# Front of a hybrid attention / SSD block: rotary tables in a pool of their own, a quarter of the first FOX weights in a lasting pool, transposes tied one tile late

## The chip, the cores and the metric

The kernel runs on one core of a Trainium2 chip. The metric is the device time of one execution in microseconds (us); the kernel before takes 2170.09 us (median of 3 runs, 2169.45 to 2170.87). Engines are named as the profile names them: PE is TensorE, DVE is VectorE, ACT is ScalarE, POOL is GpSimd, SPq is the queue on which every DMA of this kernel is issued. Each engine works through its own instruction list in order and waits where an operand or a buffer is not ready.

## The reference

One layer, 1024 tokens of width 1024, float32. The change lies in the front: the norm, the low-rank projections of the latent attention (MLA), its per-head q, k and v, and the projections of the forgetting attention (FOX) and of z.

```python
hn = rms_norm(x, norm_mix_g[l])
u = hn @ w_in[l]                       # split into u_mla (672), u_fox (1544), u_ssm, u_gate
# latent attention, before its softmax
c_q, c_kv, k_rope = jnp.split(u, [384, 640], axis=-1)
q  = (rms_norm(c_q, q_norm_g) @ w_uq).reshape(B, S, 8, 96)
kv = (rms_norm(c_kv, kv_norm_g) @ w_ukv).reshape(B, S, 8, 128)
k_nope, v = jnp.split(kv, [64], axis=-1)
k = jnp.concatenate([k_nope, broadcast(k_rope)], axis=-1)
q = rope_tail(rms_norm(q, q_gain), cos, sin)
k = rope_tail(rms_norm(k, k_gain), cos, sin)
# forgetting attention, before its softmax
q, k, v, f_raw = jnp.split(u, [512, 1024, 1536], axis=-1)
q = rms_norm(q.reshape(B, S, 8, 64), q_gain)
k = rms_norm(k.reshape(B, S, 8, 64), k_gain)
# SSD branch: z, xBC, dt_raw = split(u_ssm); its output is multiplied by silu(z)
...
```

The three branches are then attended or scanned, gated, merged and projected, and a gated MLP with a depthwise convolution follows. None of that is touched.

## The kernel before

Every fp32 product is made of three fp32r matmuls: each operand is split into a high part (ACT copies it, rounding to fp32r) and a low part (DVE subtracts the high part from the source), and `mm3` (L156) issues high x high, high x low, low x high for each of the 128-row slices k of the contraction. A weight is therefore loaded (`raw`), split by ACT and DVE, and only then used.

Tokens are handled in NT = 8 tiles of 128. The front has these stages.

Stage 1, loop at L366, over tiles t. `norm_tile` (L171) normalizes tile t+2, transposes it on PE (`pt`, 8 transposes) and splits it into `hnh`, `hnl`. Then 24 matmuls make `cq` (384 columns) and 24 make `ckv` (312 columns). ACT squares them, DVE makes the two reciprocal roots and writes the normalized row `cn` (L391, L393; one buffer). Five PE transposes of `cn` (L398, in groups of 3 and 2) go to `ch[t]`, `cl[t]`. In the iteration t = 5, `rope_and_columns` (L218) computes the rotary tables on POOL from `rt` tiles and loads and transposes four parameter blocks through one `pr` buffer (`pcp`, `pcn`). Its tiles come from the pool `ap`, which also holds `xt`, `xn`, `xg` and the gain.

PSUM has 8 banks here: 4 with the tag `mm`, 2 with `mv`, 2 with `tp`. `cq`, `ckv`, `q`, `kv` take `mm`; all the transposes take `tp`; the two `tp` buffers go round in the order of the program text.

Between the stages the pool `ap` closes and `upp`, the pool of the MLA up-projection weights (`uqh`, `uql`, `ukh`, `ukl`), takes its place on the right side of SBUF. Its raw pieces pass through five `raw` buffers of stage 1 (L341).

Stage 2, loop at L446: for each tile 18 matmuls give `q`, 12 give `kv`. ACT evacuates and squares them (`sq`, `sqk`), DVE reduces and makes the roots, POOL applies the rotation, and 16 PE transposes (L495) yield the rows that are stored to DRAM (`q_h`, `q_l`, `k_h`, `k_l`).

Stage 3, loop at L505: the FOX v columns in two halves of 256. Each half loads its weights (`load_cols`, one buffer set) and does 24 matmuls for each tile into an `mv` bank. ACT and DVE split the result into `fv` (one buffer), which is stored (`fv_d`, L514). The scheduler interleaves the first half's matmuls with stage 2.

Stage 4, loop at L636: 32 units of 24 matmuls of 512 columns, in the order z first half, FOX q, FOX k, z second half, 8 tiles each. `load512` (L613) fills `w5h`, `w5l` in four pieces of two k slices each through two `wr` buffers of the pool `fill`, which opens at L517 on the right side where `upp` was. A z unit ends in a tanh and a store; a q or k unit in a square, a reduction, the reciprocal root (`fv8`, `fr8`), the product `fqn` and four PE transposes (L668).

After that come the two attentions with their fill work (lines 683 to 1240), the merge and output projection, and the MLP.

The order on each engine up to the end of the merge is not written out: a list scheduler with a timeline simulation decides at compile time which ready instruction an engine takes next, and that order is then fixed. Pools opened with `reuse_waits="tile"` make a tile wait only for the earlier tiles whose bytes it takes over. In the allocation of the kernel before, `ukl` lies on bytes of `xg` and of the rotary tables, and the first `wr` buffer lies on bytes of the two `sl` tiles of stage 2.

Of the kernel before, what the change touches and what calls it, by code (L numbers as in the profile page):

```python
# [21 lines left out]
P = 128  # L22
# [15 lines left out]
def f32(ap):  # L38
    return ap.bitcast(F32)
# [3 lines left out]
def block_kernel(ctx: ExitStack, tc: tile.TileContext, x, positions, norm_mix_g, w_in, b_gate,  # L43
# [83 lines left out]
    def uid(s):  # L127
        cnt[0] += 1
        return f"{s}_{cnt[0]}"

    def split(h, l, src, he=None, le=None):
# [5 lines left out]
            he.tensor_copy(h, src)  # L137
        le.tensor_sub(l, src, f32(h))  # L138

    def rsqrt(pool, y, v, n):  # L140

        yi = pool.tile([P, n], I32, name=uid("rs_i"), tag="rs_i")
        V.tensor_single_scalar(yi, v.bitcast(I32), 1, op=ALU.logical_shift_right)
        V.tensor_scalar(y.bitcast(I32), yi, -1, RSQRT_MAGIC, op0=ALU.mult, op1=ALU.add)
        vh = pool.tile([P, n], F32, name=uid("rs_v"), tag="rs_v")
        V.tensor_scalar_mul(vh, v, -0.5)
        for _ in range(3):
            t = pool.tile([P, n], F32, name=uid("rs_t"), tag="rs_t")
            if n == 1:
                V.scalar_tensor_tensor(out=t, in0=y, scalar=y, in1=vh, op0=ALU.mult, op1=ALU.mult)  # L150
            else:
                V.tensor_mul(t, y, y)
                V.tensor_mul(t, t, vh)
            V.scalar_tensor_tensor(out=y, in0=t, scalar=1.5, in1=y, op0=ALU.add, op1=ALU.mult)

    def mm3(ps, lh, ll, rh, rl, nk):  # L156

        n = 3 * nk
        i = 0
        for k in range(nk):  # L160
            for a, b in ((lh, rh), (lh, rl), (ll, rh)):
                T.matmul(ps, a(k), b(k), start=(i == 0), stop=(i == n - 1))  # L162
                i += 1


    def alloc_hn():
# [163 lines left out]
    with ExitStack() as p0:  # L330
        mp = p0.enter_context(TP("mp0", 2))
        pa = ExitStack()
        ap_ = pa.enter_context(TP("ap", 2, side="right"))
        xts = []
        gmix = None

        def wsplit(pool, tag, shape, pieces):
            h = pool.tile(shape, F32R, name=tag + "h", tag=tag + "h", bufs=1)
# [27 lines left out]
        for t in range(NT):  # L366
            if t + 3 < NT:
                load_x(t + 3)
            if t + 2 < NT:
                norm_tile(ap_, "xn", mp, psp, xts[t + 2], gmix, hnh, hnl, t + 2, "tp")  # L370
            if t == NT - 3:
                rope_and_columns(ap_)
            th, tl = tok(hnh, t), tok(hnl, t)
            p1 = acc("cq")
            mm3(p1[:, :384], th, tl, lambda k: w1h[:, k, :], lambda k: w1l[:, k, :], NK)
            p2 = acc("ckv")
            mm3(p2[:, :312], th, tl, lambda k: w2h[:, k, :], lambda k: w2l[:, k, :], NK)
# [12 lines left out]
            cn = mp.tile([P, 640], F32, name=uid("cn"), tag="cn", bufs=1)  # L390
            V.scalar_tensor_tensor(out=cn[:, 0:384], in0=p1[:, :384], scalar=r[:, 0:1], in1=gcq,  # L391
                                   op0=ALU.mult, op1=ALU.mult)
            V.scalar_tensor_tensor(out=cn[:, 384:640], in0=p2[:, :256], scalar=r[:, 1:2], in1=gckv,  # L393
                                   op0=ALU.mult, op1=ALU.mult)
            for k0, k1 in ((0, 3), (3, 5)):
                pt = tps()
                for k in range(k0, k1):
                    T.transpose(pt[:, k - k0, :], cn[:, k * P:(k + 1) * P], ident)  # L398
# [22 lines left out]
    with ExitStack() as pm:  # L421
# [21 lines left out]
            eng.tensor_add(dst[:, :, 16:32], t3, t4)  # L443

        vcols = [load_cols(fvp, "v", C_FQ + 1024, 256, 1)]
        for t in range(NT):  # L446

            qn = mp.tile([P, 8, 96], F32, name=uid("qn"), tag="qn")
# [8 lines left out]
            for i in range(2):  # L457
                p = acc("kv")
                c0 = 512 * i
                mm3(p, lambda k: ch[t][:, 3 + k, :], lambda k: cl[t][:, 3 + k, :],  # L460
                    lambda k: ukh[:, k, c0:c0 + 512], lambda k: ukl[:, k, c0:c0 + 512], 2)
                pv_ = p.rearrange("p (h d) -> p h d", d=P)
                hs = slice(4 * i, 4 * i + 4)
                A.activation(kv[:, hs, :], pv_[:, :, 0:64], AF.Copy)
                split(vv[:, hs, 0:64], vv[:, hs, 64:128], pv_[:, :, 64:128])
# [2 lines left out]
            A.activation(sq, qn, AF.Square)  # L468
            ssq = mp.tile([P, 16], F32, name=uid("ssq"), tag="ssq")
            V.reduce_sum(ssq[:, 0:8], sq, axis=AX)  # L470
# [20 lines left out]
            for src, col, dsts in ((qn, gq_col, (q_h, q_l)), (kn, gk_col, (k_h, k_l))):  # L491
                for g in range(2):
                    pt = tps()
                    for j in range(4):
                        T.transpose(pt[:96, j, :], src[:, 4 * g + j, :], ident)  # L495
                    sh = mp.tile([96, 4, P], F32R, name=uid("sh"), tag="sh")
                    sl = mp.tile([96, 4, P], F32R, name=uid("sl"), tag="sl")
                    A.activation(sh, pt[:96, :, :], AF.Copy, scale=col)
                    V.scalar_tensor_tensor(out=sl, in0=pt[:96, :, :], scalar=col, in1=f32(sh),
                                           op0=ALU.mult, op1=ALU.subtract)  # L500
                    for dst, st in zip(dsts, (sh, sl)):
                        SY.dma_start(dst[4 * g:4 * g + 4, :, t * P:(t + 1) * P].rearrange("h d s -> d h s"), f32(st))


        for c0 in (0, 256):  # L505
            if c0:
                vcols.append(load_cols(fvp, "v", C_FQ + 1024 + c0, 256, 1))
# [102 lines left out]
    with ExitStack() as px:  # L610
        xp = px.enter_context(TP("xp", 2))

        def load512(c0):  # L613
            h = xp.tile([P, NK, 512], F32R, name=uid("w5h"), tag=f"w5h{units // NT % 2}", bufs=1)
            l = xp.tile([P, NK, 512], F32R, name=uid("w5l"), tag=f"w5l{units // NT % 2}", bufs=1)
            for k in range(0, NK, 2):
                raw = fpl.tile([P, 2, 512], F32, name=uid("raw"), tag="wr")
                SY.dma_start(raw, w_inv[:, k:k + 2, c0:c0 + 512])
                split(h[:, k:k + 2, :], l[:, k:k + 2, :], raw)
            return h, l  # L620

        def down_sums(k):

# [8 lines left out]
            SY.dma_start(wsum_d[k, :, 0:2, :], s12)  # L632
            SY.dma_start(wsum_d[k, :, 2:4, :], s34)

        units = 0
        for which in (3, 0, 1, 4):  # L636
            if which == 0:
                gate_sums()
# [2 lines left out]
            for t in range(NT):  # L641
                if units % 5 in (1, 3) and units // 5 * 2 + units % 5 // 2 < NFH:
                    down_sums(units // 5 * 2 + units % 5 // 2)
                p = acc("fx", "mv" if units % 3 == 2 else "mm")
                units += 1
                mm3(p, tok(hnh, t), tok(hnl, t), lambda k: wh[:, k, :], lambda k: wl[:, k, :], NK)
                if which > 2:
                    th = xp.tile([P, 512], F32, name=uid("th"), tag="fsq")
                    A.activation(th, p, AF.Tanh, scale=0.5)
# [4 lines left out]
                else:  # L654
# [10 lines left out]
                                 r.unsqueeze(2).to_broadcast([P, 8, 64]))  # L665
                    pt = tps()
                    for j in range(4):
                        T.transpose(pt[:, j, :], qn[:, 2 * j:2 * j + 2, :].rearrange("p h d -> p (h d)"), ident)  # L668
# [962 lines left out]
```

## Time and profile before

| what | value |
|---|---|
| median of 3 runs | 2170.09 us (2169.45 to 2170.87) |
| the profiled execution | 2167.16 us, its span 2165.3 us |
| mean granted TensorE clock | 0.985 |
| PE busy in the span | 2061.2 us, 95% |
| DVE, ACT, POOL busy | 1415.1, 950.9, 673.9 us |
| HBM traffic | 208.51 MB read, 92.67 MB written |

Times in the views count from the start of the span. A row of the timeline has the start, the busy time, the engine, the source line, the operation with its output and inputs, and in brackets how long the engine sat idle before it and what ended that. The end of a matmul is modelled, so successive matmuls overlap in their rows and the distance between starts is their real pace. A row of the wait view has who waited for whom, the total in us, how often, and the longest. In the table by windows the number in parentheses counts instructions; PEclk is the clock granted to TensorE as a share of full speed; DMA is the mean busy share of the 16 DMA engines.

### The profile page before, as it was taken

What the parts mean: (1) busy time and instruction counts of PE and PEld (TensorE: products, weight loads), DVE (VectorE), ACT (ScalarE), POOL (GpSimd) and SP (SyncE); (2) the same over time, 40 slices, a digit from 0 to 9 for tenths busy, and PEclk for the clock granted to TensorE, in tenths of its full rate; (3) what the DMA queues carried; (4) which work ended last, traced back from release to release, by engine and by line L of the source; (5) the groups of instructions that cost most, each with busy time, mean ns of one, the idle gap of its engine ahead of it and who ended that gap; (6) DMA issues with size and microseconds to landing.
All of it is one profiled execution on the core that took longest, in us unless ns stands there. A gap on an engine that the chain in (4) does not pass through costs nothing. (4 is left out here: it accounts for less than half of the span.)

```text
span 2165.3 us, 29068 instructions
## 1 busy us (share of the span) xinstructions
PE 2061.2 (95%) x10221; PEld 1690.6 (78%) x10221; DVE 1415.1 (65%) x2574; ACT 950.9 (44%) x1701; POOL 673.9 (31%) x626
## 2 busy tenths in 40 slices
PE   7999899999999999999999799999899999999999
PEld 6898687778888787787777688777678888887887
DVE  6686378266666676666887346457886677765665
ACT  5554232155555555555555223223444444444432
POOL 2453222222212122222220030002454554431755
PEclk9999999999999999999999899999999999999999
DMA  5167678644434354424333455341122222238665
GB/s 167 36 199 222 228 220 239 212 122 128 123 114 120 103 137 118 114 72 142 113 113 99 161 194 183 109 138 58 58 88 78 78 88 78 78 119 310 238 217 187
DMA packets 275610, 303.10 MB, mean 140 GB/s; under 512 B 19292, under 2 KB 208744, under 8 KB 275464
## 3 DMA queue, kind: packets, MB, share of 16 engines
q1 hardware_dynamic: 275464, 301.24, 45.2%
q8 instruction: 81, 1.33, 0.3%
q14 instruction: 65, 0.53, 0.1%
HBM read 208.51 MB, written 92.67 MB: 139 GB/s over the span
## 5 line engine op out<-in xcount | busy, mean ns | idle before, releaser
L789 PE MATMUL mm<-hnh,wh 128*128 128x512 f32 x576 | 242.7, 421 | 0.0
L902 POOL TENSOR_SCALAR pm<-pm,rs 128x128 f32<-128x128 f32 (+7 forms) x128 | 109.5, 858 | 404.2 <-DVE rs L901 258.2
L789 PE MATMUL mm<-hnl,wh 128*128 128x512 f32 x576 | 228.6, 397 | 0.0
L789 PE MATMUL mm<-hnh,wl 128*128 128x512 f32 x576 | 228.5, 397 | 0.0
L1578 PE MATMUL dn<-dr,dr 128*128 128x512 f32 x616 | 191.6, 393 | 0.5 <-DVE dr L138 0.5
L895 ACT ACTIVATE pm<-s,nmx 128x128 f32<-128x128 f32 (+2 forms) x192 | 110.1, 578 | 97.7 <-DVE nmx L892 70.0
L954 DVE TENSOR_TENSOR ptl<-tp,pth 128x512 fp32r<-128x512 f32 (+1 forms) x160 | 100.2, 632 | 70.0 <-ACT pth L953 68.6
L885 DVE TENSOR_REDUCE nmx<-s 128x1 f32<-128x128 f32 (+2 forms) x192 | 105.6, 553 | 56.7 <-PE s L883 44.8
L1578 PEld LDWEIGHTS dn<-dr,dr 128*128 128x128 f32 x616 | 116.9, 190 | 25.3 <-DVE dr L138 1.0
L880 PE MATMUL s<-qk,qk 96*128 96x384 f32 (+5 forms) x480 | 121.4, 357 | 11.3 <-ACT pm L895 10.0
L953 ACT ACTIVATE pth<-tp 128x512 fp32r<-128x512 f32 (+1 forms) x160 | 88.0, 553 | 99.6 <-PE tp L948 99.1
L789 PEld LDWEIGHTS mm<-hnh,wl 128*128 128x128 f32 x576 | 109.4, 190 | 25.6
L789 PEld LDWEIGHTS mm<-hnh,wh 128*128 128x128 f32 x576 | 110.3, 191 | 18.1 <-issue 2.9
L1578 PE MATMUL dn<-dr 128*128 128x512 f32 x308 | 121.2, 394 | 2.7 <-ACT dr L135 2.7
L789 PEld LDWEIGHTS mm<-hnl,wh 128*128 128x128 f32 x576 | 110.0, 191 | 15.8 <-issue 0.2
L138 DVE TENSOR_TENSOR dr<-dr,dr 128x1024 fp32r<-128x1024 f32 x55 | 80.1, 1458 | 55.3 <-ACT dr L135 48.1
L162 PE MATMUL fx<-w5h,hnh 128*128 128x512 f32 x256 | 102.9, 406 | 7.3 <-ACT w5h L135 7.3
L135 ACT ACTIVATE wh<-wr 128x1024 fp32r<-128x1024 f32 (+1 forms) x46 | 41.9, 911 | 152.8 <-PE ybr L162 74.5
L162 PE MATMUL ybr<-ah,wh 128*128 128x512 f32 x256 | 101.1, 400 | 1.6 <-ACT ah L135 1.6
L162 PE MATMUL fx<-w5h,hnl 128*128 128x512 f32 x256 | 102.5, 402 | 0.0
L162 PE MATMUL fx<-w5l,hnh 128*128 128x512 f32 x256 | 102.3, 401 | 0.0
L880 PEld LDWEIGHTS s<-qk,qk 96*128 96x128 f32 (+1 forms) x480 | 81.7, 193 | 24.9 <-ACT pm L895 14.7
(441 smaller groups left out, 5791.6 us busy)
## 6 DMA issues: line engine op xcount, KB each, us to landing
dr<-act_d SPq DMA_DIRECT2D x99, 256.0 KB
wr<-in_ffn_w_up_dram SPq DMA_DIRECT2D x46, 512.0 KB
wr<-in_w_in_dram SPq DMA_DIRECT2D x36, 512.0 KB
g_d<-t SPq DMA_DIRECT2D x24, 512.0 KB
gl<-g_d SPq DMA_DIRECT2D x24, 512.0 KB
ws<-in_ffn_w_down_dram SPq DMA_DIRECT2D x22, 512.0 KB
wsum_d<-ws SPq DMA_DIRECT2D x22, 512.0 KB
act_d<-fa SPq DMA_DIRECT2D x22, 512.0 KB
```

The source lines that it names most:

```text
L135: A.activation(h, src, AF.Copy)
L138: le.tensor_sub(l, src, f32(h))
L162: T.matmul(ps, a(k), b(k), start=(i == 0), stop=(i == n - 1))
L789: T.matmul(ps, a[:, k, :], b[half][:, k, :], start=(k == 0 and i == 0), stop=(k == NK - 1 and i == 2))
L880: T.matmul(ps[:, :w], q_[:, qs], k_[:, a:a + w], start=i_ == 0, stop=not last and i_ == len(o.passes) - 1)
L885: later(c + 0.1, lambda ps=ps, ci=ci, a=a, b=b: V.reduce_max(nmx[:, ci:ci + 1], ps[:, :b - a], axis=AX, negate=True))
L895: pss[ci][1][0] = later(c + 0.9 + 0.1 * ci, lambda ci=ci, a=a, b=b: A.activation(p_[:, a:b], pss[ci][0][:, :b - a], AF.Exp, bias=nb, accum ...
L902: G.tensor_scalar(p_[:, 0:n * P], p_[:, 0:n * P], rs[:, 3:4], 0.0, op0=ALU.mult, op1=ALU.add)
L953: later(c + 0.05, lambda th=th, pt=pt, off=off: A.activation(th[:, :off], pt[:, :off], AF.Copy))
L954: pl[0] = later(c + 0.6, lambda th=th, tl=tl, pt=pt, off=off: V.tensor_sub(tl[:, :off], pt[:, :off], f32(th[:, :off])))
L1578: T.matmul(ps[m], a[:, ts_], b[:, 512:], start=first_ and k == 0 and q == 0, stop=k == NFH - 1 and q == 2, skip_group_check=not first_)
```

## The change

It does these things.

- `rope_and_columns` takes its tiles from a new pool `rpp`, opened in stage 1 on the left side behind `mp0`, in place of `ap`.
- A new pool `fill3` of 8 KB in each partition is opened on the right side between the closing of `ap` and the opening of `upp`, and stays to the end. After stage 3 it is filled with the k slices 0 and 1 of the first z weights, in two pieces of 256 KB through the `vr` buffers of stage 3. `load512` then loads only three of the four pieces for the first eight units.
- The first six z units start with the six matmuls of k = 0 and 1 (`head`), in six PSUM banks, before any of them goes on with k = 2 to 7.
- `late(a, b)` adds an order edge without a wait: instruction a is placed behind instruction b on its engine. It ties the first transpose of a tile in stages 1 and 2, and of a q or k unit in stage 4, behind the last matmul of the next tile or unit. The last tile of stages 1 and 2 stays untied.
- In stage 2 `sqk` shares the single buffer of `sq`.
- The DMA scratch at the start of each partition is 1 KB instead of the 16 KB of the default. All left pools move down by 15 KB, and the right pools other than `fill3` by 8 KB.

```diff
+    def late(a, b):
+
+        if a is not None:
+            tc.add_manual_dep(a.ins, b.ins.name, mybir.DependencyInfo(
+                mybir.DependencyClass.NoSync, mybir.DependencyReason.DATA), reason="late")
...
         ap_ = pa.enter_context(TP("ap", 2, side="right"))
+        rpp = p0.enter_context(TP("rpp", 1))
...
             if t == NT - 3:
-                rope_and_columns(ap_)
+                rope_and_columns(rpp)
...
-            mm3(p2[:, :312], th, tl, lambda k: w2h[:, k, :], lambda k: w2l[:, k, :], NK)
+            m = mm3(p2[:, :312], th, tl, lambda k: w2h[:, k, :], lambda k: w2l[:, k, :], NK)
+            late(held0, m)
...
-                    T.transpose(pt[:, k - k0, :], cn[:, k * P:(k + 1) * P], ident)
+                    i = T.transpose(pt[:, k - k0, :], cn[:, k * P:(k + 1) * P], ident)
+                    if k == 0:
+                        held0 = i
...
         pa.close()
+        fp3 = ctx.enter_context(TP("fill3", 1, side="right"))
         upp = pmla.enter_context(TP("upp", 1, side="right"))
...
+                m = mm3(p, lambda k: ch[t][:, 3 + k, :], lambda k: cl[t][:, 3 + k, :],
+                        lambda k: ukh[:, k, c0:c0 + 512], lambda k: ukl[:, k, c0:c0 + 512], 2)
+                if i == 1:
+                    late(held0, m)
...
-            sqk = mp.tile([P, 8, 64], F32, name=uid("sqk"), tag="sqk", bufs=1)
+            sqk = mp.tile([P, 8, 96], F32, name=uid("sqk"), tag="sq", bufs=1)[:, :, 0:64]
...
-                        T.transpose(pt[:96, j, :], src[:, 4 * g + j, :], ident)
+                        i = T.transpose(pt[:96, j, :], src[:, 4 * g + j, :], ident)
+                        if src is qn and g == 0 and j == 0:
+                            held0 = i
...
+        w0 = [fp3.tile([P, 2, 512], F32R, name=uid(n), tag=n) for n in ("wh", "wl")]
+        for k in range(2):
+            raw = fvp.tile([P, 512], F32, name=uid("raw"), tag="vr", bufs=2)
+            SY.dma_start(raw, w_inv[:, k, C_Z:C_Z + 512])
+            split(w0[0][:, k, :], w0[1][:, k, :], raw)
     pmla.close()
...
-            for k in range(0, NK, 2):
+            for k in range(0 if units else 2, NK, 2):
                 raw = fpl.tile([P, 2, 512], F32, name=uid("raw"), tag="wr")
...
+        def part(p, t, k0, k1):
+            th, tl = tok(hnh, t), tok(hnl, t)
+            for k in range(k0, k1):
+                for i, (a, b) in enumerate(((th, wh), (th, wl), (tl, wh))):
+                    m = T.matmul(p, a(k), b(k), start=k == 0 and i == 0, stop=k == NK - 1 and i == 2)
+            return m
...
-                p = acc("fx", "mv" if units % 3 == 2 else "mm")
+
+                if units == 0:
+                    head = [acc("fx", "mv" if i % 3 == 2 else "mm") for i in range(6)]
+                    for i in range(6):
+                        part(head[i], i, 0, 2)
+                p = head[t] if units < 6 else acc("fx", "mv" if units % 3 == 2 else "mm")
+                m = part(p, t, 2 if units < 6 else 0, NK)
                 units += 1
-                mm3(p, tok(hnh, t), tok(hnl, t), lambda k: wh[:, k, :], lambda k: wl[:, k, :], NK)
+                late(held0, m)
+                held0 = None
...
-                        T.transpose(pt[:, j, :], qn[:, 2 * j:2 * j + 2, :].rearrange("p h d -> p (h d)"), ident)
+                        i = T.transpose(pt[:, j, :], qn[:, 2 * j:2 * j + 2, :].rearrange("p h d -> p (h d)"), ident)
+                        if j == 0:
+                            held0 = i
...
-    nc = _bacc.Bacc("TRN2", target_bir_lowering=False, num_devices=1)
+    nc = _bacc.Bacc("TRN2", target_bir_lowering=False, num_devices=1, dynamic_dma_scratch_size=1024)
```

More of the change, by code (lines that the diff above doesn't have):

```diff
@@ L161, in mm3 @@
             for a, b in ((lh, rh), (lh, rl), (ll, rh)):
-                T.matmul(ps, a(k), b(k), start=(i == 0), stop=(i == n - 1))
+                m = T.matmul(ps, a(k), b(k), start=(i == 0), stop=(i == n - 1))
                 i += 1
+        return m
     def alloc_hn():
@@ L445, in block_kernel @@
         vcols = [load_cols(fvp, "v", C_FQ + 1024, 256, 1)]
+        held0 = None
         for t in range(NT):
@@ L459, in block_kernel @@
                 c0 = 512 * i
-                mm3(p, lambda k: ch[t][:, 3 + k, :], lambda k: cl[t][:, 3 + k, :],
-                    lambda k: ukh[:, k, c0:c0 + 512], lambda k: ukl[:, k, c0:c0 + 512], 2)
+                m = mm3(p, lambda k: ch[t][:, 3 + k, :], lambda k: cl[t][:, 3 + k, :],
+                        lambda k: ukh[:, k, c0:c0 + 512], lambda k: ukl[:, k, c0:c0 + 512], 2)
+                if i == 1:
+                    late(held0, m)
                 pv_ = p.rearrange("p (h d) -> p h d", d=P)
@@ L619, in load512 @@
                 split(h[:, k:k + 2, :], l[:, k:k + 2, :], raw)
-            return h, l
+            if units:
+                return [lambda k, e=e: e[:, k, :] for e in (h, l)]
+            return [lambda k, e=e, f=f: f[:, k, :] if k < 2 else e[:, k, :] for e, f in zip((h, l), w0)]
         def down_sums(k):
@@ L633, in down_sums @@
             SY.dma_start(wsum_d[k, :, 2:4, :], s34)
-        units = 0
+        def part(p, t, k0, k1):
[3 more added lines that the diff above has]
+                    m = T.matmul(p, a(k), b(k), start=k == 0 and i == 0, stop=k == NK - 1 and i == 2)
+            return m
+        units, held0 = 0, None
         for which in (3, 0, 1, 4):
@@ L643, in block_kernel @@
                     down_sums(units // 5 * 2 + units % 5 // 2)
-                p = acc("fx", "mv" if units % 3 == 2 else "mm")
+                if units == 0:
[4 more added lines that the diff above has]
+                m = part(p, t, 2 if units < 6 else 0, NK)
                 units += 1
-                mm3(p, tok(hnh, t), tok(hnl, t), lambda k: wh[:, k, :], lambda k: wl[:, k, :], NK)
+                late(held0, m)
+                held0 = None
                 if which > 2:
```

## The prediction

> **What bounds the kernel now.** I read the page first, then who waited for PE's operands in the first 640 us, then the busy time by stage, and last the timelines of the two worst places.
>
> ```profile
> span 2165.3 us, 29068 instructions
> PE 2061.2 (95%) x10221; PEld 1690.6 (78%) x10221; DVE 1415.1 (65%) x2574; ACT 950.9 (44%) x1701; POOL 673.9 (31%) x626
> ```
>
> PE is busy for 95% of the span, so PE's idle time and its slow clock are what can be won; the other engines matter where they make it wait. The edits end before the attentions, so the front's share of that idle time is the stake:
>
> ```profile
> PE pt L193 <- DVE xn L187: 8.9, 1, 8.9
> PE fx L162 <- ACT w5h L135: 7.3, 1, 7.3
> PE tp L398 <- DVE cn L391: 6.7, 2, 3.8
> PE tp L668 <- DVE fv L660: 3.8, 2, 2.0
> PE fxv L162 <- DVE fv L138: 3.6, 5, 1.4
> PE tp L668 <- DVE fqn L664: 1.3, 1, 1.3
> ```
>
> 8.9 us is the start of the program, which no edit touches. The largest wait inside is for the first FOX weights (7.3), then the transposes of `cn` (6.7 in two waits), then those of the FOX units (3.8 and 1.3).
>
> ```profile
> 92.60:104.40 11.80, 7.44 (x35) 6.17 (x34) 10.19 (x35) 8.58 (x29) 0.00 (x0) 0.86 0.36 108
> 100.00:180.00 80.00, 77.07 (x502) 72.07 (x502) 69.70 (x192) 46.81 (x103) 43.80 (x106) 1.00 0.64 193
> 180.00:217.00 37.00, 32.00 (x249) 29.25 (x246) 22.55 (x51) 15.76 (x28) 7.98 (x15) 1.00 0.81 236
> 217.00:229.00 12.00, 4.75 (x12) 3.75 (x12) 7.52 (x19) 2.76 (x5) 0.00 (x0) 0.72 0.37 122
> ```
>
> Between stages 1 and 2 (92.6 to 104.4) PE idles 4.4 us and runs at a clock of 0.86; between stages 3 and 4 (217 to 229) it idles 7.25 us at 0.72. Stage 2 is full. In stage 3 DMA is busy for 0.81 of the time.
>
> **The change part by part: the quarter in `fill3`.**
>
> ```profile
> 216.75 0.28 PE L162 MATMUL fxv<-v,hnl 128*128 128x256 f32 x1
> 224.28 2.93 PE L162 MATMUL fx<-w5h,hnh 128*128 128x512 f32 x6 [7.25 <-ACT w5h L135]
> 227.00 0.63 PE L162 MATMUL fx<-w5l,hnh 128*128 128x512 f32 x1
> 227.43 0.63 PE L162 MATMUL fx<-w5h,hnl 128*128 128x512 f32 x1
> 229.31 0.40 PE L162 MATMUL fx<-w5l,hnh 128*128 128x512 f32 x1
> ...
> 230.72 0.40 PE L162 MATMUL fx<-w5l,hnh 128*128 128x512 f32 x1
> ...
> 222.90 0.38 ACT L135 ACTIVATE fv<-fxv 128x256 fp32r<-128x256 f32 x1 [2.50 <-DMA fv_d<-fv]
> 223.18 1.99 ACT L135 ACTIVATE w5h<-raw 128x1024 fp32r<-128x1024 f32 x2
> 229.27 1.06 ACT L135 ACTIVATE w5h<-raw 128x1024 fp32r<-128x1024 f32 x1 [4.10 <-DMA raw<-in_w_in_dram]
> ...
> 212.33 0.89 SPq L618 DMA_DIRECT2D raw<-in_w_in_dram  x2
> 225.83 14.53 SPq L618 DMA_DIRECT2D raw<-in_w_in_dram  x6
> ...
> 220.33 0.42 DVE L138 TENSOR_TENSOR fv<-fxv,fv 128x256 fp32r<-128x256 f32 x1 [1.67 <-ACT fv L135]
> ```
>
> PE ends stage 3 at 217.03 (224.28 less 7.25). The split it waits for is queued on ACT behind the last `fv` split, which itself waits for the store of the `fv` before. Then eleven matmuls (the 12 of the window 217 to 229 less the last `fxv`) run at 0.43 us (227.00 to 227.43) where the pace is 0.235 (229.31 to 230.72 in six steps): 11 x 0.195 = 2.1 us. At stake: 7.25 + 2.1 = 9.35 us.
>
> [...]
>
> The new split is two pieces of 128x512, loaded through the v buffers that are free after the second half's weights; in stage 3 ACT is busy for 15.76 of 37 us, so it finds a place before 217. Then `head` has 36 x 0.235 = 8.5 us of work. Banks bind next: heads 2 and 5 need the two `mv` banks, which DVE frees at 220.33 + 0.42 = 220.75 and, behind ACT's 222.90, at about 223.7. Heads 0 and 1 last until 217.03 + 2.8 = 219.8, a wait of 0.9 follows, heads 2 to 4 last until 224.95, head 5 until 226.35. By then k = 2 to 5 are split even at the old times (223.18 + 1.99 on ACT, and if DVE takes as long as ACT's 1.06, 226.2). Best: 9.35 - 0.9 = 8.4 us. If k = 6, 7 come as late as now (third load at 225.83, split 229.27 + 2 x 1.06 = 231.4) and PE goes unit by unit, PE waits 231.4 - (226.35 + 12 x 0.235) = 2.2: 6.2 us. This can improve too: `fill` moves 8 KB down and `mp` 15 KB, so the `wr` buffers leave the bytes of `sl`, whose last stores precede 212.33; the loads can be issued earlier. That is also the price: 0.5 MB of `fill3` and up to 0.5 MB more go out before 217, next to the `fv` stores that set the chain:
>
> ```profile
> ACT fv L135 <- DMA fv_d<-fv: 20.3, 7, 5.1
> ```
>
> At 236 GB/s, 1 MB is 4.4 us; 0.19 x 37 = 7 us of DMA time is spare there. So 0 to 4.4 us off: 1.8 to 8.4 us in all. I take 7.0, near the upper end, because the spare time exceeds the moved bytes.
>
> **The rotary tables in `rpp`.**
>
> ```profile
> 32.77 2.79 SPq L343 DMA_DIRECT2D raw<-in_mla_w_uq_dram  x5
> 94.11 2.21 ACT L135 ACTIVATE uqh<-raw 128x384 fp32r<-128x384 f32 x5
> 96.74 5.04 SPq L343 DMA_DIRECT2D raw<-in_mla_w_ukv_dram  x8
> 93.90 0.76 PE L398 MATMUL tp<-ident,cn 128*128 128x128 f32 x5 [0.61 <-ACT pc_f L304]
> 95.47 1.03 PE L162 MATMUL q<-uqh,ch 128*128 128x384 f32 x2 [0.80 <-DVE cn L391]
> 103.39 0.61 DVE L391 SCALAR_TENSOR_TENSOR cn<-cq,r,gcq 128x384 f32<-128x384 f32 x1
> 104.15 0.52 PE L398 MATMUL tp<-ident,cn 128*128 128x128 f32 x3 [2.93 <-DVE cn L391]
> ```
>
> The first five pieces of the up-projection were issued at 32.8 and split only at 94.1, all fourteen splits fall between 94 and 105, on ACT and on DVE, and the last `cn` (103.39) is queued among them; PE waits 2.93 us for it. With the tables out of `ap` and `upp` moved down, `uqh` lies on no tile of `ap` and the rest on `xt`, `xn` and the gain, which stage 1 leaves before its end. The splits then go into stage 1 (ACT is busy for 44% of the span) and the wait of 2.93 goes. The other two stay: 0.61 and 0.80 come from the single `pr` buffer (its transposes hold the two `tp` buffers in front of `cn`), which is the same in `rpp`. The slow clock after them stays as well: (1 - 0.86) x 11.8 = 1.7 us. Bounds: 0 if the scheduler keeps the splits where they are, 2.93 + 0.61 + 0.80 + 1.7 = 6.0 if all goes. I take 3.0, the one wait whose cause is removed.
>
> **The order one tile late.** Is it there already? Matmuls issued before the first transpose of a tile:
>
> ```profile
> L162 PE MATMUL ckv<-w2l,hnh 128*128 128x312 f32 x16 | 4.8, 312 | 0.0
> 37.81 0.84 PE L398 MATMUL tp<-ident,cn 128*128 128x128 f32 x3 [3.78 <-DVE cn L391]
> ...
> L162 PE MATMUL kv<-ukl,ch 128*128 128x512 f32 x12 | 4.7, 393 | 0.0
> 126.26 0.27 PE L495 MATMUL tp<-ident,qn 128*96 128x128 f32 x1
> ...
> L162 PE MATMUL fx<-w5l,hnh 128*128 128x512 f32 x90 | 35.7, 401 | 0.0
> 291.82 0.38 PE L668 MATMUL tp<-ident,fqn 128*128 128x128 f32 x2
> ```
>
> Stage 1: 16 products of low weights, 8 for each tile, so tiles 0 and 1 are complete when tile 0 is transposed. Stage 2: 12 at 4 for each tile, so three tiles before the transposes of tile 0. Stage 4: 90 at 8 for each unit, 11.25 units, where the first q unit is the ninth. The edges ask for one tile; the order has one to two. So they cost and bring nothing: 0, for all three loops. The wait of 3.78 at 37.81 stays also because four `mm` banks hold tiles 0 and 1 until `cn` is written; nothing else could start. If an edge did bind, it would put a transpose up to one unit later (24 x 0.235 = 5.6 us), with `fqn` and its banks queued behind; if the waits of the FOX units came from early transposes, 3.8 + 1.3 = 5.1 us would go. Both are rivals below.
>
> **`sq` shared.** ACT's second square now waits for DVE's first reduction:
>
> ```profile
> L470 DVE TENSOR_REDUCE ssq<-sq 128x8 f32<-128x768 f32 x8 | 7.6, 946 | 2.8 <-ACT sq L468 2.8
> ACT kv L464 <- DVE kn L481: 3.7, 1, 3.7
> ```
>
> At least 0.95 us for each tile if DVE takes it at once, 3.7 (ACT's longest wait on DVE here) if not, and behind it on ACT are the copies that free PSUM banks. ACT is busy for 46.81 of 80 us and the transposes come two tiles late: I take 0, with 8 x 0.95 = 7.6 to 8 x 3.7 = 29.6 us if that cover is gone. The scratch and the pool addresses: 0.
>
> **The sum.** 7.0 + 3.0 = 10 us. Behind the front the lists are PE's, so it carries to the end: 2167.2 (the profiled execution, 1.9 us around its span) becomes 2157. The profiled execution was 2.9 us under the median of the runs, so the forecast is 2170.1 - 10 = 2160 us. Its own range is 2170.1 - 8.4 - 6.0 = 2156 to 2170.1 - 1.8 - 3.0 = 2165.3.
>
> **The rivals.** (a) Nothing gained at the FOX weights: ACT's list has the new splits behind the last `fv` split, as the old ones now, or the moved loads hold up the stores by the whole 4.4 us and PE finds no bank. For it: 20.3 us of ACT's waits are for these stores. Against: ACT has the idle time, and 36 matmuls then lack only two banks. It leaves at most the 3.0: about 2168 us.
> (b) The explicit order decides: the waits of the FOX units (5.1 us) go as well. For it: they are waits of in-order transposes. Against: those transposes are already more than a unit late. 2160 - 5 = 2155 us.
> (c) Slower: the shared `sq`. ACT stands in stage 2 until DVE, 87% busy there (69.70 of 80), comes to the reduction; `q` banks and `tp` buffers are freed later and PE, now full (77.07 of 80), stands each time. In the middle of 0.95 and 3.7, 2.3 us for each tile: 8 x 2.3 = 18 us, 2178 us. It decides from 10 / 8 = 1.25 us for each tile. For it: DVE's load. Against: DVE took the `sq` reductions with only 2.8 us idle before eight of them, so mostly its list stood ready.
>
> **How the numbers follow.** Forecast 0.55, (a) 0.15, (b) 0.14, (c) 0.16. The time is 2160 us. The range is 2151 (b with the upper bound of `rpp`: 2170.1 - 8.4 - 6.0 - 5.1) to 2172, which holds (a) and leaves out most of (c). About 0.2% (4.3 us, 2165.8 to 2174.4) is what can be told from no change: faster 0.55 + 0.14 + 0.02 of (a) = 0.71, same 0.13, slower 0.16.
>
> **What would show it.** Right: a wait before the first `fx` matmul under 2 us instead of 7.25, and PEclk near 1.0 around it; splits of `uqh` before 90 us, and no wait of 2.9 us before the last `cn` transpose; the waits before L668 as before. Wrong: `wh` splits behind the last `fv`; longer waits of ACT on DMA at `fv`; ACT waiting at L472 on DVE; idle PE in stage 2; or waits that grow behind 430 us, where I expect the same order moved forward.

## The result, and the profile after

The changed kernel takes 2174.82 us (median, 2169.93 to 2179.91) where the kernel before, measured beside it, takes 2169.89 us: a ratio of 1.0019 with a 95% interval of 1.0012 to 1.0027, so 4.1 us slower (2.6 to 5.9). The forecast was 2160 us, and 2174.8 lies above its range. The first attention, which no edit touches, starts at 439.2 us instead of 431.0 in the profiled executions, and what follows is as long as before (1735.0 and 1734.3 us): the loss is in the front.

The lines have moved: L398 is now L408 (transposes of `cn`), L304 is L311 (copies of the columns), L660 to L668 are L699 to L707 (FOX), and the products of the FOX units are at L664. The head of the page:

```profile
span 2174.2 us, 29062 instructions
PE 2069.6 (95%) x10221; PEld 1699.9 (78%) x10221; DVE 1411.2 (65%) x2575; ACT 951.8 (44%) x1702; POOL 678.9 (31%) x626
```

PE has as many instructions as before and is busy 8.4 us longer (2061.2 before). So the loss is not mainly idle time. The waits of PE up to 440 us (engine, line, whom it waited for: us in total, times, longest):

```profile
PE tp L707 <- DVE fv L699: 6.1, 1, 6.1
...
PE tp L408 <- DVE cn L401: 4.2, 1, 4.2
PE fxv L168 <- ACT v L135: 3.6, 1, 3.6
PE fx L664 <- DVE fv L138: 3.5, 1, 3.5
PE tp L408 <- ACT pc_f L311: 2.6, 1, 2.6
PE tp L707 <- DVE fqn L703: 2.5, 2, 1.6
PE tp L707 <- DVE rs_t L158: 1.7, 1, 1.7
PE pcp L310 <- DMA pr_f<-in_ffn_conv_b_dram: 1.1, 1, 1.1
```

The wait of 7.25 us for the first FOX weights is gone, and 3.5 is left of it. In its place stand 6.1 us before a FOX transpose (longest before: 2.0), 3.6 for v weights, and 2.6 and 1.1 at the columns. The clock shows what such waits cost beyond themselves. From 100 to 200 us, first before, then after (length, busy us of PE, PEld, DVE, ACT and POOL with their instructions, PE's clock, DMA share, GB/s):

```profile
100.00:200.00 100.00, 94.57 (x634) 87.62 (x633) 84.58 (x225) 56.98 (x121) 51.78 (x120) 1.00 0.70 207
```

```profile
100.00:200.00 100.00, 93.62 (x584) 87.50 (x585) 77.64 (x209) 52.28 (x112) 47.08 (x112) 0.94 0.63 190
```

PE is busy as long and gets through 584 instructions instead of 634, at a clock of 0.94 instead of 1.00. Summed over windows of 10 us up to the first attention, three terms make its start: idle time, busy time times (1 - clock), and the rest, which is the work at full clock.

| profiled run | first attention | idle | slow clock | rest |
|---|---|---|---|---|
| before | 431.0 | 36.5 | 6.0 | 388.5 |
| after | 439.2 | 39.9 | 13.1 | 386.2 |

Of the 8.2 us, 3.4 are idle time and 7.1 slow clock, and the rest gives 2.3 back. Three places show where it goes.

**Between stages 1 and 2.** ACT, SP's queue and PE in the changed kernel (start, us, engine, line, operation, output<-input; in brackets the idle time before it and who ended it):

```profile
87.33 2.20 ACT L135 ACTIVATE uqh<-raw 128x384 fp32r<-128x384 f32 x5
...
93.61 1.15 ACT L135 ACTIVATE ukh<-raw 128x256 fp32r<-128x256 f32 x3 [1.64 <-DMA raw<-in_mla_w_ukv_dram]
94.67 0.23 ACT L311 ACTIVATE pc_f<-pcp 128x88 f32<-128x88 f32 x1
...
98.33 0.24 ACT L311 ACTIVATE pc_f<-pcp 128x88 f32<-128x88 f32 x1
```

```profile
89.71 3.45 SPq L352 DMA_DIRECT2D raw<-in_mla_w_ukv_dram  x5
...
93.64 0.34 SPq L308 DMA_DIRECT2D pr_f<-in_ffn_conv_b_dram  x1
```

```profile
95.59 0.27 PE L310 MATMUL pcp<-ident,pr_f 88*128 88x88 f32 x1 [1.15 <-DMA pr_f<-in_ffn_conv_b_dram]
...
98.62 1.32 PE L408 MATMUL tp<-ident,cn 128*128 128x128 f32 x5 [2.60 <-ACT pc_f L311]
100.64 0.69 PE L168 MATMUL q<-uqh,ch 128*128 128x384 f32 x1 [0.71 <-DVE cn L401]
101.13 0.52 PE L168 MATMUL q<-uql,ch 128*128 128x384 f32 x1
101.45 0.52 PE L168 MATMUL q<-uqh,cl 128*128 128x384 f32 x1
```

ACT and SP's queue at the same place in the kernel before:

```profile
90.71 0.24 ACT L304 ACTIVATE pc_f<-pcp 128x88 f32<-128x88 f32 x1 [4.70 <-PE pcp L303]
...
93.61 0.24 ACT L304 ACTIVATE pc_f<-pcp 128x88 f32<-128x88 f32 x1
```

```profile
91.05 0.35 SPq L301 DMA_DIRECT2D pr_f<-in_ffn_conv_b_dram  x1
```

The splits of `uqh` moved forward by seven microseconds, as forecast. But those of `ukh` came along, and on ACT they stand, waiting for their pieces, ahead of the first copy of the columns: 94.67 instead of 90.71. The rest of ACT's list follows behind it, with the sine and cosine of the rotary tables. So the second copy comes at 98.33 instead of 93.61, the transposes of `cn` behind it at 98.62 instead of 93.90, and the first q product at 100.64 instead of 95.47. On SP the second pair of loads through the one `pr` buffer, which PE's transpose frees, stands behind five of the new pieces: its last goes out at 93.64, not 91.05, and PE waits 1.15 us for it. The changed kernel comes to this place 1.6 us late (the first transpose of the columns is at 87.04 instead of 85.44), so 3.6 of the 5.2 us arise here. And the q products then go at 0.32 us each, until about 105, where the pace is 0.175: clock 0.5.

**Stage 4, the weights.** The third piece of the k weights on SP and ACT, and DVE and PE at the place of the 6.11:

```profile
334.81 0.43 SPq L641 DMA_DIRECT2D raw<-in_w_in_dram  x1
```

```profile
341.41 1.06 ACT L135 ACTIVATE w5h<-raw 128x1024 fp32r<-128x1024 f32 x1 [8.46 <-DMA raw<-in_w_in_dram]
```

```profile
342.50 1.23 DVE L138 TENSOR_TENSOR w5l<-raw,w5h 128x1024 fp32r<-128x1024 f32 x1 [4.13 <-ACT w5h L135]
...
344.04 1.28 DVE L158 TENSOR_TENSOR rs_t<-fr 128x8 f32<-128x8 f32 x1
345.35 1.19 DVE L159 TENSOR_TENSOR rs_t<-rs_t,rs_v 128x8 f32<-128x8 f32 x1
346.57 0.17 DVE L160 SCALAR_TENSOR_TENSOR fr<-rs_t,fr 128x8 f32<-128x8 f32 x1
```

```profile
349.63 1.09 PE L707 MATMUL tp<-ident,fqn 128*128 128x128 f32 x4 [6.11 <-DVE fv L699]
```

The same transpose in the kernel before, where the piece was issued at 329.04:

```profile
341.38 0.63 PE L668 MATMUL tp<-ident,fqn 128*128 128x128 f32 x4 [1.76 <-DVE fv L660]
```

DVE has the low part of that piece in the middle of a reciprocal root and stands 4.13 us for it; behind it, three operations of 8 elements take 1.1 to 1.3 us instead of 0.17. PE's transpose waits for all of that. The wait is put down to `fv` at L699 (the tile `fv8` of the root, since the rows leave buffer numbers out; it is not the v tile of stage 3). The rows show two causes in its place: the late load, and the long operations, which are some 3.1 of the 6.11 us (1.28 + 1.19 + 1.12 - 3 x 0.17).

**Stage 4, POOL's sums.** They stand beside exactly those long operations:

```profile
344.03 1.26 POOL L654 TENSOR_TENSOR ws<-ws,ws 128x512 f32<-128x512 f32 x1 [4.00 <-DMA ws<-in_ffn_w_down_dram]
345.25 1.26 POOL L655 TENSOR_TENSOR ws<-ws,ws 128x512 f32<-128x512 f32 x1
```

### The profile page after: what moved, and what is told of

Read it like the earlier page. It is cut to its first block, busy times and chain, and to the rows that moved or that the text cites. A ratio compares the mean times of both kernels' runs of the same rounds, so it can differ in the third digit from the quotient of the medians.

```text
span 2174.2 us, 29062 instructions
## 1 busy us (share of the span) xinstructions
PE 2069.6 (95%) x10221; PEld 1699.9 (78%) x10221; DVE 1411.2 (65%) x2575; ACT 951.8 (44%) x1702; POOL 678.9 (31%) x626
## 5 line engine op out<-in xcount | busy, mean ns | idle before, releaser
L138 DVE TENSOR_TENSOR dr<-dr,dr 128x1024 fp32r<-128x1024 f32 x55 | 74.6, 1357 | 59.9 <-ACT dr L135 54.9
L921 PEld LDWEIGHTS s<-qk,qk 96*128 96x128 f32 (+1 forms) x480 | 83.0, 195 | 24.1 <-ACT pm L936 13.7
L168 PE MATMUL ybr<-al,wh 128*128 128x512 f32 x256 | 100.8, 396 | 0.0
L168 PE MATMUL ybr<-ah,wl 128*128 128x512 f32 x256 | 100.6, 395 | 0.0
L664 PE MATMUL fx<-w5h,hnh 128*128 128x512 f32 x240 | 96.5, 407 | 0.0
```

The source lines that it names most:

```text
L168: m = T.matmul(ps, a(k), b(k), start=(i == 0), stop=(i == n - 1))
L664: m = T.matmul(p, a(k), b(k), start=k == 0 and i == 0, stop=k == NK - 1 and i == 2)
L921: T.matmul(ps[:, :w], q_[:, qs], k_[:, a:a + w], start=i_ == 0, stop=not last and i_ == len(o.passes) - 1)
```

## The experiments

Every ratio is against the kernel before, run on the same chip between the runs shown. "Quarter" is the quarter of the weights with the head, "tables" the rotary tables in `rpp`, "square" the shared buffer. All kernels below have the changed kernel's smaller DMA scratch.

**The explicit order taken out.**

```diff
-        if a is not None:
+        if False:
```

> The changed kernel without the explicit order (the helper adds no edge). Theory P (the edges ask for less delay than the order already has, and cost nothing): the same lists on every engine, so the time of the changed kernel, 2174.8 us within 3. Rival (the order moved the FOX transposes and made the wait of 6.1 us before one of them): 2169, and no wait over 3 us before a FOX transpose.

Without the edges the instructions of every engine stand in the same order as with them, so this is the changed kernel a second time: 1.0035 (1.0021 to 1.0050), first attention at 439.55, idle time 40.5 and slow clock 12.9, a wait of 5.26 before a FOX transpose. The edges asked for what the order had. The two ratios also show how far two measurements of one program can lie apart, 0.16%.

**One part undone.** Tables back:

```diff
-        rpp = p0.enter_context(TP("rpp", 1))
...
-                rope_and_columns(rpp)
+                rope_and_columns(ap_)
```

> The changed kernel with the rotary tables and columns back in the pool of stage 1. Theory P (the early splits of the up-projection stand ahead of the copies of the columns and hold PE between stages 1 and 2): the first q matmul at about 96 us instead of 100.6, the first transpose of qn at about 126 instead of 133.4, the quarter's gain of about 5 us stays, so 2165 to 2170. Rival S (the shared square buffer costs the time in stage 2): the q matmul earlier but the time still 2173 to 2176. Rival F (FOX gives back whatever comes early): 2173 to 2176 with a longer wait before a FOX transpose.

0.9995 (0.9983 to 1.0008), the time of the first theory. The first q product is at 97.22, the waits at the columns are again one of 0.72, and the 3.04 before the last transposes of `cn` is back. Before the FOX transposes PE waits 10.7 us, in the changed kernel 10.3.

The quarter undone (weights loaded whole, no `head`):

```diff
...
-            for k in range(0 if units else 2, NK, 2):
+            for k in range(0, NK, 2):
...
-                p = head[t] if units < 6 else acc("fx", "mv" if units % 3 == 2 else "mm")
-                m = part(p, t, 2 if units < 6 else 0, NK)
+                p = acc("fx", "mv" if units % 3 == 2 else "mm")
+                m = part(p, t, 0, NK)
```

> The changed kernel with the first FOX weights loaded whole, as before (no quarter, no head). Theory P (the quarter wins about 5 us between stages 3 and 4): 2179 to 2181, with a wait of over 6 us before the first FOX matmul. Rival F (the quarter's loads or the shift by it cause the longer waits in FOX, 10.3 us in place of 5.0): 2174 to 2176 with FOX waits of about 5 us.

1.0015 (1.0005 to 1.0025): no slower than with the quarter. The wait before the first FOX product is 6.47 again, and the waits before the FOX transposes fall to 5.8. The wait of the first theory came out, and the time and the shorter waits of the rival: the quarter does win its time, and FOX does take it back.

The squares apart:

```diff
-            sqk = mp.tile([P, 8, 96], F32, name=uid("sqk"), tag="sq", bufs=1)[:, :, 0:64]
+            sqk = mp.tile([P, 8, 64], F32, name=uid("sqk"), tag="sqk", bufs=1)
```

> The changed kernel with a buffer of its own for the second square. Theory P (the shared buffer costs nothing, since PE is not waiting in stage 2): 2174.8 within 2. Rival S (ACT stands for DVE in stage 2): 2167 to 2170, with the period of the qn transposes below the 10.5 us of both kernels.

1.0006 (0.9994 to 1.0018), between what the two theories asked for; first q at 99.95, waits before the FOX transposes 11.3.

**One part alone**, with the other parts undone by the edits above and no edges. Quarter:

> The kernel before with the quarter and the head alone (tables in the pool of stage 1, squares apart, no edges). Theory G (the quarter wins some 7 us until the 192nd product of a FOX unit, and FOX gives 6 to 9 us back, 10 us of waits before its transposes where the kernel before has 5): ratio 0.999 to 1.001. Rival K (the quarter's gain is kept, what FOX lost came from the tables): 2163 to 2166, ratio 0.997, with FOX waits of about 5 us.

0.9983 (0.9969 to 0.9997): a gain of 3.7 us (0.7 to 6.7), between the two theories. From the first q product to the 192nd product of a FOX unit it takes 266.8 - 97.6 = 169.2 us where the kernel before takes 271.1 - 95.5 = 175.6: 6.4 us won. From there to the first attention it takes 167.5 instead of 159.9: in the profiled executions 7.6 us are given back. Waits of PE there, and the third k piece on SP and ACT:

```profile
285.09 0.33 PE L626 MATMUL tp<-ident,cum 128*128 128x128 f32 x1 [1.46 <-DVE Fl L138]
...
291.64 0.63 PE L706 MATMUL tp<-ident,fqn 128*128 128x128 f32 x4 [1.80 <-DVE rs_t L158]
...
344.77 1.09 PE L706 MATMUL tp<-ident,fqn 128*128 128x128 f32 x4 [5.85 <-DVE fv L698]
```

```profile
329.93 0.43 SPq L640 DMA_DIRECT2D raw<-in_w_in_dram  x1
```

```profile
336.56 1.06 ACT L135 ACTIVATE w5h<-raw 128x1024 fp32r<-128x1024 f32 x1 [7.69 <-DMA raw<-in_w_in_dram]
```

PE is 4.3 us ahead of the kernel before at the 192nd product. Over the first two waits, which the kernel before does not have, the lead falls to 0.6 us, and where PE comes to wait for the third piece it is 0.7 us ahead (338.92 for 339.62). The piece itself comes later: it has one of two buffers, stands on SP behind the loads and stores of the weight sums (329.93 for 329.04), and its split is at 336.56 for 334.16. So PE waits 5.85 us for 1.76.

Tables:

> The kernel before with the rotary tables in their own pool alone. Theory P (the early splits of the up-projection stand ahead of the copies of the columns): first q matmul at 100 instead of 95.5, ratio 1.002 to 1.004, 2175 to 2180. Rival S (the shared buffer of the squares costs the time, not the tables): ratio 0.999 to 1.001.

1.0020 (1.0007 to 1.0032). The first q product is at 101.17, behind the same two waits, of 1.29 and 2.81 us.

Square:

> The kernel before with the shared square buffer alone. Theory A (ACT's second square waits for DVE's first sum, some 0.95 us or less for each of eight tiles, partly on the path): ratio 1.001 to 1.002. Rival N (nothing, as PE has work in stage 2): 0.999 to 1.001.

1.0011 (0.9998 to 1.0025), not told from nothing. ACT does wait at the second square (the waits of ACT in stages 2 and 3):

```profile
ACT sqk L486 <- DVE ssq L484: 7.7, 5, 1.7
```

These are 7.7 us in five waits, none over 1.7; the changed kernel has 2.2 us of them, and no wait of PE in stage 2 ends on it. The three parts sum to 0.20 + 0.11 - 0.17 = 0.14%, and the changed kernel measures 0.19 and 0.35: the parts add up within their intervals.

**The boundary.** The changed kernel with the splits of `uk` ordered behind the last copy of the columns:

```diff
+    def hold(a, b):
+        tc.add_manual_dep(b.ins, a.ins.name, mybir.DependencyInfo(
+            mybir.DependencyClass.NoSync, mybir.DependencyReason.DATA), reason="late")
...
-            A.activation(dst, pt, AF.Copy)
+            cols.append(A.activation(dst, pt, AF.Copy))
...
-                split(h[:, k, c0:c1], l[:, k, c0:c1], raw[:, 0:c1 - c0])
+                i = A.activation(h[:, k, c0:c1], raw[:, 0:c1 - c0], AF.Copy)
+                if tag == "uk":
+                    hold(cols[-1], i)
+                V.tensor_sub(l[:, k, c0:c1], raw[:, 0:c1 - c0], f32(h[:, k, c0:c1]))
```

> The changed kernel with an order that puts the eight splits of the second up-projection on ACT behind the last copy of the columns. Theory P (these splits, waiting for their pieces, stand ahead of the copies and hold PE between stages 1 and 2): the wait before the transposes of cn near 98 us falls from 2.6 to under 1, first q matmul at 96 to 98, 2 to 4 us less than the changed kernel at the 192nd product, ratio 1.000 to 1.002. Rival (the columns come late by their own chain of loads through the single buffer, whatever the splits do): first q matmul at 99.5 to 101 and no gain.

```profile
96.69 0.77 PE L416 MATMUL tp<-ident,cn 128*128 128x128 f32 x5 [0.95 <-ACT pc_f L315]
98.29 0.69 PE L172 MATMUL q<-uqh,ch 128*128 128x384 f32 x1 [0.83 <-DVE cn L409]
```

```profile
93.40 0.34 SPq L312 DMA_DIRECT2D pr_f<-in_ffn_conv_b_dram  x1
```

The 2.60 falls to 0.95 and q starts 2.4 us earlier. All the profiled kernels show what this place costs: from the first transpose of the columns to the first q product it takes 10.0 us in each of the seven without the tables in a pool of their own, 13.4 to 14.0 in the eight with them, and 11.5 to 11.9 in the three with the splits held as well (this one and two below). So the splits on ACT were the cause of about half of the 3.6 us. The cause of the other half is not shown: the last load through `pr` still stands on SP behind five of the pieces (93.40 here), and no run changed that order. The time is 1.0004 (0.9992 to 1.0016), some 3 us under the changed kernel, though the intervals overlap. Part comes back as a longer wait for v weights in stage 3 (4.61 for 3.63), whose cause stays open.

**FOX.** Four raw buffers instead of two in the changed kernel:

```diff
-                raw = fpl.tile([P, 2, 512], F32, name=uid("raw"), tag="wr")
+                own = k % 4 == 2 if units else k == 6
+                raw = (xp if own else fpl).tile([P, 2, 512], F32, name=uid("raw"), tag="w5r" if own else "wr", bufs=2)
```

> The changed kernel with four buffers instead of two for the raw pieces of the FOX weights. Theory L (the third raw piece of the k weights is loaded late, DVE holds its split inside the reciprocal root and PE stands 5 to 6 us): that wait falls under 2 us, the waits of FOX from 10 to about 5, 2169 to 2171. Rival C (the waits come from POOL's sums, beside which the small operations of DVE take 1.2 us instead of 0.17): the wait near 349 us stays over 3 us and the time within 2 us of the changed kernel.

0.9979 (0.9967 to 0.9990), 0.4% under the changed kernel and faster than the kernel before. All four pieces are out by 284.4 us (the third at 334.81 in the changed kernel), and their splits stand in one row:

```profile
281.22 3.21 SPq L642 DMA_DIRECT2D raw<-in_w_in_dram  x3
```

```profile
319.53 3.90 ACT L135 ACTIVATE w5h<-raw 128x1024 fp32r<-128x1024 f32 x4
```

Of the waits before FOX transposes 8.1 us are left, the longest 3.56. That is less than expected; the slow clock fell with them, from 13.1 to 8.9 us.

The sums of units 6 to 23 on DVE, in the changed kernel (one of four lines):

```diff
-            G.tensor_sub(s12[:, 0, :], w1[:, 1, :], w1[:, 0, :])
+            (V if 6 <= units < 24 else G).tensor_sub(s12[:, 0, :], w1[:, 1, :], w1[:, 0, :])
```

> The changed kernel with the subtractions of the weight sums on DVE instead of POOL in units 6 to 23. Theory C (POOL's sums hold DVE's small operations of the reciprocal roots): no operation of 8 elements over 0.5 us between 285 and 390 us, the wait of 1.7 us near 296 goes and the one near 349 falls by about 3, 2170. Rival L (only the late raw piece counts, and DVE has four operations of 0.7 us more for each sum): the wait near 349 stays over 5 us, 2175 or more.

0.9987 (0.9976 to 0.9998). The operations of 8 elements between 285 and 392 us, first in the changed kernel, then here (count | busy us, mean ns | idle before):

```profile
L158 DVE TENSOR_TENSOR rs_t<-fr 128x8 f32<-128x8 f32 x47 | 16.5, 351 | 1.4
```

```profile
L158 DVE TENSOR_TENSOR rs_t<-fr 128x8 f32<-128x8 f32 x48 | 7.7, 165 | 1.1
```

With the sums off POOL the mean halves, and the waits at 296 and 349 us go. So both causes are real, and either cure alone gives the changed kernel 0.3% or more.

Is the late piece the change's own? The four buffers in the kernel before:

> The kernel before with four buffers for the raw pieces of the FOX weights. Theory L (the late piece is the change's own loss: before, PE waits only 2 us for it): ratio 0.998 to 1.000. Rival (the pieces are late in both kernels and the four buffers win the same anywhere): 0.995 to 0.997.

0.9983 (0.9971 to 0.9996). They win here too, so the rival holds in part: the changed kernel wins 0.4% by them, the kernel before 0.17%. The profiled executions do not show where, as FOX takes 159.9 us before and 159.2 here. The one of before, 2167.2 us, is near the fast end of its runs; that the piece is late in many others is likely, and not shown.

**Together.** Quarter, four buffers and sums on DVE; the same with the tables; and that with the splits held:

> The kernel before with the quarter and the head, four raw buffers for the FOX weights and the sums of units 6 to 23 on DVE; tables in the pool of stage 1, squares apart. Theory L and C together (the late piece and POOL's sums took back the quarter's gain): waits before FOX transposes under 4 us in all, ratio 0.994 to 0.996, 2160 to 2164. Rival (FOX is bound by its transfers, and gives back whatever comes early): ratio 0.998 as with the quarter alone.

> The same with the tables in their own pool. Theory P (the tables cost some 4 us at the boundary of stages 1 and 2): ratio 0.002 above that of the kernel without them (0.996 to 0.998). Rival (their cost was a matter of FOX's phase and goes with its waits): the same ratio within 0.001.

> The kernel with tables, quarter, four raw buffers and sums on DVE, and the splits of the second up-projection held behind the copies of the columns. Theory P: first q matmul at 96 to 98, ratio 0.001 to 0.002 below that without the hold, about that of the kernel without the tables. Rival: no difference within 0.001.

0.9982 (0.9966 to 0.9997), 0.9990 (0.9978 to 1.0002) and 0.9980 (0.9965 to 0.9994): the signs are as expected and the intervals overlap, so the steps of 0.1% aren't shown. The first missed: with the sums on DVE as well it is no better than the quarter alone.

Quarter and four buffers, and the changed kernel with the splits held and four buffers:

> The kernel before with the quarter, the head and four raw buffers. Theory L (the quarter's 0.17% plus the wait of 5.9 us given back, less what POOL's sums hold): ratio 0.995 to 0.997. Rival (FOX gives back what comes early, by another wait): 0.998.

> The changed kernel with the splits held and four raw buffers. If the causes add up: 0.15% or more under the changed kernel with four raw buffers alone (0.9979), so 0.9955 to 0.997. Rival (the hold's gain is swallowed in stage 3, where PE then waits for the v weights): 0.998.

0.9963 (0.9948 to 0.9978) and 0.9971 (0.9956 to 0.9986). The second is 0.08% under the changed kernel with four buffers, less than the 0.15% that was expected. The first is the fastest: 2166.92 us beside 2174.44 for the kernel before. The gains of the two parts alone add up (0.17 + 0.17). Its longest waits at the head and before the FOX transposes of q are

```profile
226.03 0.50 PE L664 MATMUL fx<-wh,hnh 128*128 128x512 f32 x1 [1.36 <-DVE fv L138]
...
336.32 0.63 PE L707 MATMUL tp<-ident,fqn 128*128 128x128 f32 x4 [2.73 <-DVE rs_t L159]
```

The terms of the profiled runs, as above, with the length of FOX (from the start of the 192nd product to the first attention):

| run | first attention | idle | slow clock | FOX | ratio |
|---|---|---|---|---|---|
| after | 439.2 | 39.9 | 13.1 | 166.2 | 1.0019 |
| tables alone | 442.0 | 42.1 | 13.7 | 164.0 | 1.0020 |
| square alone | 439.7 | 41.8 | 9.2 | 163.2 | 1.0011 |
| quarter alone | 434.3 | 39.7 | 7.1 | 167.5 | 0.9983 |
| four raw buffers alone | 432.7 | 36.7 | 8.6 | 159.2 | 0.9983 |
| quarter, four raw buffers | 424.2 | 32.9 | 4.1 | 160.0 | 0.9963 |

FOX takes 166.2 to 169.0 us in the six profiled runs with the quarter, two raw buffers and POOL's sums, and 159.9 to 164.0 in the four of these without the quarter. A single execution can lie some us off the median: by the ratios the quarter wins 0.17% with two buffers and 0.20% (0.9963 against 0.9983) with four, so they do not show that the four buffers save more where the quarter is. What of its 6.4 us FOX takes back on average, and so how much of it the late piece is, stays open.

## Why the prediction was wrong

**The step that failed first** is the rotary tables, put at 3.0 us won. That the splits go into stage 1 and the wait of 2.93 goes held: `uqh` is split at 87.3, and a wait of 0.71 is left. "The other two stay: 0.61 and 0.80 come from the single `pr` buffer" did not. The splits that moved forward moved past the copies of that chain on ACT and past its loads on SP, and lengthened it to 1.15 + 2.60 us. The moved splits and loads were counted, but not which of the instructions they pass PE waits for. The tables alone measure 0.20% (0.07 to 0.32): 4.4 us lost where 3.0 were to be won. The stretch to the first q product is 3.6 us longer, and holding the splits back on ACT takes about half of that away.

**The second** is a sentence of the sum: "Behind the front the lists are PE's, so it carries to the end." The quarter's term was near, 7.0 forecast and 6.4 in the trace of the quarter alone, and PE does wait for banks in the head, 0.81 + 1.34 us (0.9 was foreseen); not foreseen was that 22 of the 36 products of the head run among the v products of stage 3. But FOX lies between it and the end, and in that execution PE's lead goes there in three waits: 1.46 and 1.80 us near 285 and 292, and 5.85 instead of 1.76 for a piece that comes 2.4 us later than before. Measured to the end, 3.7 us arrive (0.7 to 6.7). By the parts, the tables are 7.4 us above their term, the quarter 3.3 and the square 2.4: 13.1 of the 14.1 us between -10 and the measured +4.1.

**The slow clock** was in the sum only where a wait was to go. Its loss up to the attention grew from 6.0 to 13.1 us, more than the idle time did: a wait of 7.25 was exchanged for several of 1 to 6 us, with spells of half pace behind them (PEclk 0.50 from 101 to 104, 195 to 201, 233 to 236 and 350 to 354 us).

**Right**: the edges at 0, for the reason given (the same order without them). The wait at the start of the front (3.78) stays: 4.19, and 3.78 or 3.79 in most runs. **Not told**: the square, put at 0, measures 0.11% (-0.02 to 0.25); ACT's waits of 7.7 us are near the lower bound's 7.6, but in five waits and not eight; the 18 us of rival (c) are excluded, so that (c) came nearest in time (2178) is luck. Of (a) the part about PE finding no bank is in the 3.5 us left before the first FOX units; (b) fell with the edges. The smaller scratch, put at 0 without a reason, is in every kernel run here and was not run by itself. Why the v weights come late in the runs with the tables (PE waits 1.4 to 1.5 us for ACT's split of them with the squares apart, 2.7 to 3.9 with the square shared) stays open.

## What to carry to other kernels

When a step becomes free to start earlier, list what it passes on each in-order engine and queue, and ask whether the bound engine waits for any of that; an order that holds it behind those few instructions can keep part of the gain (it took away about half of the added stretch here). A gain ahead of a stage can be given back inside it: follow PE's lead through that stage product by product to the waits where it goes, and cure those in the same change (four buffers for a late load brought 0.17 to 0.4% here). Count a wait with the slow clock behind it: here one of 7.25 us gave way to several of 1 to 6 us, and the loss to the slow clock rose from 6.0 to 13.1 us.

## What the runs showed of the hardware

In the changed kernel DVE operations of 8 elements took 0.15 to 0.17 us while POOL stood idle (296 to 312 us), and 1.28, 1.19 and 1.12 us beside POOL's subtractions of 128x512 (DVE from 344.04 and POOL from 344.03 us in the rows above); each of the three ended within 0.03 us of the subtraction beside it. Moving the sums off POOL took the mean of the first of these operations, L158, from 351 to 165 ns.

The clock fell in the changed kernel behind waits of 1.15 and 2.60 us with half a microsecond of transposes between, and stayed at half until about 105 us, some 6.5 us from 98.6 (windows of the changed kernel, columns as above):

```profile
98.00:101.00 3.00, 1.67 (x6) 1.28 (x7) 2.27 (x11) 2.53 (x13) 0.57 (x3) 0.61 0.58 166
101.00:104.00 3.00, 3.00 (x10) 3.00 (x10) 2.58 (x11) 0.00 (x0) 2.39 (x11) 0.50 0.05 17
```

Behind waits of 3.78 and 3.79 us near 38 us it was back within the second window in the kernel before, and only after it, at about 44.4 us, with the quarter alone:

```profile
38.00:41.00 3.00, 3.00 (x11) 3.00 (x11) 2.71 (x16) 1.53 (x2) 0.70 (x1) 0.50 0.02 5
41.00:44.00 3.00, 3.00 (x19) 2.93 (x19) 2.90 (x7) 0.29 (x1) 1.69 (x1) 0.95 0.04 18
```

```profile
38.00:41.00 3.00, 1.93 (x7) 1.96 (x8) 2.74 (x16) 1.02 (x2) 0.00 (x0) 0.50 0.26 83
41.00:44.00 3.00, 3.00 (x11) 3.00 (x11) 2.93 (x8) 0.51 (x1) 2.38 (x1) 0.50 0.00 0
```

The spell at half pace varies: about 3.4 us in the kernel before (37.81 to 41.2), 5.3 with the quarter alone (39.07 to 44.4), 6.5 in the changed kernel (98.6 to 105). And the waits of 1.15 and 2.60 us, with only transposes between them, were followed by such a spell as the single ones of 3.78 and 3.79 were.
